# Token mixing's weight loads and masks issued ahead of the layer norm, and four expected waits reset

## The chip, the cores and the metric

The kernel runs on one core of one Trainium2 chip. The metric is the device time of one execution in microseconds (us); the median of three runs of the kernel before is 1336.76 us (1336.02 to 1337.26). A difference of about 0.2% (2.7 us) is what a measurement of this kernel can tell from none.

## What is computed

One step of a two-layer hybrid decoder over 544 positions (a prompt of 512, and 8 decode sequences of 4). In each layer one projection feeds four head groups, whose outputs are joined and projected back; a feed-forward part with a short convolution follows.

```python
def hybrid_layer(x, pos, k_pos, st, p):
    h = rmsnorm(x, p['norm1_g'])
    proj = h @ p['w_in']
    (a_qkv, a_z, a_b, a_a, b_b, b_c, b_h, c_q, c_k, c_v, d_u, d_v) = jnp.split(proj, ...)
    ...  # A: gated DeltaNet in chunks of 64; B: gated convolution; C: window attention
    du = jax.nn.gelu(d_u)
    dvn = layernorm(jax.nn.gelu(d_v), p['d_ln_g'], p['d_ln_b'])
    out_d = chunk_token_mlp(du, dvn, p['d_ws'], p['d_bias'])   # D
    x = x + jnp.concatenate([out_a, out_b, out_c, out_d], axis=-1) @ p['w_out']
    h2 = rmsnorm(x, p['norm2_g'])
    gate, f_conv_new = causal_dwconv(st['f_conv'], h2 @ p['ffn_w_gate'], p['ffn_conv_w'])
    x = x + (jax.nn.silu(gate) * (h2 @ p['ffn_w_up'])) @ p['ffn_w_down']

def chunk_token_mlp(u, v, ws, bias):
    wm = jnp.where(jnp.tril(jnp.ones((n, n), bool)), ws[:, :n, :n], 0.0)
    mixed = jnp.einsum('gts,bcsgd->bctgd', wm, vc) + bias...
    return u * mixed.reshape(bsz, t, width)
```

The change touches head group D (token mixing): a lower-triangular mask on a 128x128 weight of each of four groups, a product with the normed v rows, a bias, and a product with gelu(u).

## The kernel before

**Projections.** Activations lie with channels on the partitions. A projection of 128 columns is eight groups over the 1024 inputs; in a group each weight tile is used as a high part `wh` and a low part `wl`, in six matmuls of 272 columns (the trace shows them as three pairs, `xh,wh`, `xl,wh`, `xh,wl`). Weights come in on SP's queue (L709), ACT makes `wh` (L745) and DVE makes `wl` (L747). In a layer the projections run in the order k0 q0 v0 cq0 cq1 ck k1 q1 v1 u0 u1 c0 h0 b0 c1 h1 b1 z0 z1, then the output projection and the feed-forward part.

**Side work between the groups.** Everything else that PE does in this stage is placed between these groups by the class `Order`. Side generators (`a00` and so on for DeltaNet by layer and head pair, `c0`/`c1` for attention, `d0`/`d1` for token mixing, `n0`/`n1` for the norm of v, `g` and `e` besides) give back either a delay in planned microseconds or the name of an event; `od.mark(name, latency)` says at which planned time an event is there, and the table `LAT` adds a wait before a given step of a generator. Planned time runs with the matmuls that are issued. So the table and the marks decide PE's order at build time. The orders of DVE, ACT, POOL and SP are set afterwards by the scheduler of the build, by its own timeline; on the chip each engine runs its list in order and waits for semaphores.

**Token mixing.** `mix_d` is spawned after projection v1 and the store of the convolution state (`o_sao`, L1598). It loads `wmt` (128x512, the weights) and masks it on POOL (L1379), loads `wm4` (32x128, for the decode rows) and masks it on POOL (L1382), and loads `dbias`. Then for each of two column tiles it computes `pmx` (16 matmuls of prompt rows, from `dvn`) and `pmd` (4 of decode rows, from `dvd`), and DVE adds the bias and multiplies by `du` (`mx_`, L1399 to L1401). `normed_dv` is a generator that normalises v in five tiles: one DVE step (L1531) and two POOL steps each (L1532, L1533), then the store `o_cvs` (L1534), and marks `dv{l}`, the event for which `mix_d` waits. It is started when the projection u0 has been scaled on DVE (L1607).

**Its neighbours.** Attention makes scores `psc` (L1348 reads them, from `ck`, whose last step is L1578), exponentials on ACT (L1260), a scaling on ACT (L1268), transposes `ptr` on PE, their copies `pt` on ACT (L1363) and the product `pov`. DeltaNet makes `pk`, `pkt`, `pvt` (which needs `kd`, L1022), `pW`, `pR` and the norms `pl`, which ACT reads at L942. `psc`, `ptr`, `pl`, `pmx`, `pmd` and `pov` share one pool of two PSUM buffers, taken in turn: a matmul into it waits until the reader of the buffer's last tile is done.

Of the kernel before, what the change touches and what calls it, by code (L numbers as in the profile page):

```python
# [273 lines left out]
def _unhost(r):  # L274
# [8 lines left out]
    def conv(a, k, n):  # L283
# [19 lines left out]

LAT = {
    "a00": {
        3: 1.60, 13: 15.62, 14: 3.75, 15: 2.87, 16: 1.87, 17: 3.23, 18: 1.78, 19: 2.03, 34: 1.52,
    },
    "a01": {
        3: 3.96, 4: 1.12, 10: 2.64, 24: 0.84,
    },  # L310
    "a10": {
        3: 1.56, 13: 15.67, 14: 3.68, 15: 2.79, 16: 3.85, 17: 1.45, 25: 1.33, 36: 0.47, 42: 1.13,
    },
    "a11": {
        3: 3.59, 6: 3.32, 13: 1.06, 28: 0.70, 35: 0.30,
    },
    "c0": {
        1: 1.19, 2: 4.34, 5: 7.17, 6: 0.65, 7: 2.67, 8: 3.40,
    },
    "c1": {  # L320
        1: 0.81, 2: 4.06, 5: 7.68, 6: 0.61, 7: 15.38, 10: 1.48,
    },
    "d0": {
        4: 6.53,
# [90 lines left out]
def _body(ctx, tc, I, O, depth=DEPTH, dump=None):  # L415
# [7 lines left out]
    od = Order()  # L423

    def mm(out, lhsT, rhs, **kw):
        k, m, n = lhsT.shape[0], lhsT.free_size(), rhs.free_size()
        if lhsT.dtype == F32R:
            c = max(n, 256) / 2400.0 + 0.0025
        else:
            c = 4 * max(n, m) / 2400.0  # L430
            if k <= 32 and m <= 32:
                c *= 0.74
            elif k <= 64 and m <= 64:
                c *= 0.72
        od.spend(c, n * k / 128.0 * (1 if lhsT.dtype == F32R else 4))
        nc.tensor.matmul(out, lhsT, rhs, **kw)  # L436
# [9 lines left out]
    def bc(ap, axis, n):  # L446
        u = ap.unsqueeze(axis)
        shp = list(u.shape)
        shp[axis] = n
        return u.to_broadcast(shp)  # L450
# [16 lines left out]
    def n5(nm, w=571):  # L467
        return p5.tile([128, w], F32, tag="w5", name=nm)

    def nx(nm, shape, dt=F32):  # L470
        return slabs.tile(shape, dt, tag="s5", name=nm)

    def ncc(nm, shape):
        return pc.tile(shape, F32, tag="c2", name=nm)
# [4 lines left out]
    def ps(nm, shape):  # L479
        return pss.tile(shape, F32, tag="ps", name=nm)  # L480
# [19 lines left out]
    def C(nm, a=None, b=None):  # L500
        o, n = _COFF[nm]
        if a is None:
            return cst[:, o:o + n]
        return cst[:, o + a:o + b]
# [8 lines left out]
    def split(src, nm):  # L513
        hi, lo = nx(nm + "h", [128, T], F32R), nx(nm + "l", [128, T], F32R)
        act(hi, src, AF.Copy)  # L515
        tt(lo, src, hi.bitcast(F32), op=ALU.subtract)  # L516
        return hi, lo
# [267 lines left out]
    def dmp(nm, ap):  # L785
        if dump is not None and nm in dump:
            nc.gpsimd.dma_start(dump[nm], ap)

    def bs(ap):
        return ap.rearrange("p (b t) -> p b t", b=DB)  # L790
# [582 lines left out]


    def mix_d(l, L):
        yield ("ev", f"dv{l}")
        wmt = nx("wmt", [128, 4, 128])
        nc.sync.dma_start(wmt, I["wmt"][l])
        pool.tensor_tensor(wmt, wmt, bc(C("tri"), 1, 4), op=ALU.mult)  # L1379
        wm4 = ncc("wm4", [32, 4, 32])  # L1380
        nc.sync.dma_start(wm4, I["wm4"][l])
        pool.tensor_tensor(wm4, wm4, bc(C("udc")[0:32], 1, 4), op=ALU.mult)  # L1382
        dbias = ncc("dbias", [128, 2, 128])
        nc.sync.dma_start(dbias, I["dbias"][l])
        for i in range(2):
            yield ("ev", f"u{l}{i}")
            pmx = ps("pmx", [128, 4, 128])
            for n in range(4):
                for a in range(2):
                    gr = 2 * i + a  # L1390
                    mm(pmx[hs[a], n], L.dvn[n // 2][:, n % 2, 64 * gr:64 * gr + 64], wmt[:, gr],
                       start=True, stop=True)
            pmd = ps("pmd", [128, ND])
            for a in range(2):
                gr = 2 * i + a
                mm(pmd[hs[a]], L.dvd[0:ND, 64 * gr:64 * gr + 64], wm4[:, gr], start=True, stop=True,
                   tile_position=(0, 64 * a))
            mx_ = n5("mx_", T)
            tt(mx_[:, 0:SEQ].rearrange("p (n t) -> p n t", n=4), pmx, bc(dbias[:, i], 1, 4), op=ALU.add)  # L1399
            tt(bs(mx_[:, SEQ:T]), bs(pmd), bc(dbias[:, i, 0:DS], 1, DB), op=ALU.add)  # L1400
            tt(mx_, mx_, L.du[i], op=ALU.mult)  # L1401
            dmp(f"od{i}", mx_)
            L.cat[6 + i] = split(mx_, f"d{i}")
            yield 1.0
        od.mark(f"catD{l}", 3.5)


    def main():
# [42 lines left out]
        for l in range(depth):  # L1451
# [53 lines left out]
            for c in range(5):  # L1505
# [5 lines left out]
                dv = dvn[c // 2][:, c % 2] if c < 4 else dvd[0:ND]  # L1511
# [15 lines left out]
            def normed_dv():  # L1527
                yield ("ev", f"nd{l}")
                with tc.issue_after(L.du_ins):
                    for c, (dv, r0) in enumerate(dvs):  # L1530
                        ts(dv, dv, mv[0:r0, c, 0:1], rs[0:r0, c:c + 1], op0=ALU.subtract, op1=ALU.mult)  # L1531
                        pool.tensor_tensor(dv, dv, lnr[0:r0, 0], op=ALU.mult)  # L1532
                        pool.tensor_tensor(dv, dv, lnr[0:r0, 1], op=ALU.add)  # L1533
                nc.sync.dma_start(O["cvs"][l], dvd[0:ND])  # L1534
                od.mark(f"dv{l}", 8.0)

            od.spawn(normed_dv(), f'n{l}')
            yield 0.0

# [60 lines left out]


            od.spawn(mix_d(l, L), f'd{l}')
            L.du = []
            for i in range(2):
# [249 lines left out]
```

## Time and profile before

| | |
|---|---|
| median of three runs | 1336.76 us (1336.02 to 1337.26) |
| profiled execution | 1336.89 us, its span 1335.1 us |
| PE busy | 1291.5 us, 97% of the span |
| DVE, ACT, POOL busy | 958.9, 647.2, 401.9 us |

The profile is of one execution. PE is TensorE's matmuls; DVE, ACT, POOL and SP are VectorE, ScalarE, GpSimd and SyncE. A timeline row gives the start, the busy time, the engine, the line, the operation and its tile names, and in brackets how long the engine had stood idle before and what released it. The span begins 1.8 us later than the time that the run was measured with, or ends so much earlier.

### The profile page before, as it was taken

The page shows a single profiled execution, that of the slowest core. Times are in us where ns is not written, and L with a number is a line of the kernel's source. Part 1 is how long each engine was busy: PE and PEld are TensorE (multiplying, and loading weights), DVE is VectorE, ACT ScalarE, POOL GpSimd, SP SyncE. Part 2 cuts the span into 40 slices and gives each one's busy share as a digit, 9 for nine tenths or more (in the row PEclk, how much of TensorE's full clock was granted, in tenths as well). Part 3 has the DMA queues.
Part 4 walks back from the last instruction along what each step waited for, and adds up shares of the span by engine and source line. Part 5 has one row for each costly group of instructions (what it writes and reads, how often), then busy time and mean ns, then how long its engine had stood idle before and what let it go on. Part 6 is the DMA issues. An engine that isn't in the chain of part 4 may idle for free.

```text
span 1335.1 us, 29979 instructions
## 1 busy us (share of the span) xinstructions
PE 1291.5 (97%) x12574; PEld 1240.5 (93%) x12574; DVE 958.9 (72%) x1565; ACT 647.2 (48%) x1142; POOL 401.9 (30%) x528
## 2 busy tenths in 40 slices
PE   8998999999999999999999989999999999999997
PEld 7987889999999999999999878889989999999997
DVE  6897943579777778876658867546796887687665
ACT  6645423455455444544545543335555454455444
POOL 2123320001655354452001142100034654643321
PEclk9998999998999999999999989999999999999999
DMA  7222241231233233233532221413312332232232
GB/s 279 99 69 65 80 133 42 89 101 58 70 101 101 84 100 102 84 95 88 162 124 101 66 75 60 124 46 98 99 52 87 92 111 86 97 99 88 89 91 73
DMA packets 48086, 125.60 MB, mean 94 GB/s; under 512 B 10144, under 2 KB 14432, under 8 KB 47824
## 3 DMA queue, kind: packets, MB, share of 16 engines
q1 hardware_dynamic: 47952, 123.70, 29.6%
q8 instruction: 98, 1.61, 0.5%
q14 instruction: 36, 0.29, 0.1%
HBM read 115.01 MB, written 8.67 MB: 93 GB/s over the span
## 4 chain that ended last, share of the span: by engine, by line
PE 81%; DVE 11%; ACT 3%; issue 2%; DMA 1%; POOL 0%; SPq 0%; DVEq 0%; ACTq 0%; POOLq 0%
PE pdn L436 17%; PE pA L436 11%; PE po L436 8%; PE pD L436 7%; PE pup L436 4%; PE pgt L436 4%; PE pB L436 4%; PE pC L436 3%; DVE wl L747 3%; PE ptm L436 2%; PE pj_b L436 2%; PE pj_z L436 2%; PE pj_c L436 2%; PE pj_h L436 2%; PE p L436 2%
## 5 line engine op out<-in xcount | busy, mean ns | idle before, releaser
L747 DVE TENSOR_TENSOR wl<-wr,wh 128x1024 fp32r<-128x1024 f32 (+4 forms) x218 | 257.6, 1182 | 91.0 <-ACT wh L745 89.7
L745 ACT ACTIVATE wh<-wr 128x1024 fp32r<-128x1024 f32 (+4 forms) x218 | 194.1, 890 | 197.6 <-PE pA L436 31.0
L436 PE MATMUL pdn<-hdh,wh 128*128 128x272 f32 x684 | 142.3, 289 | 8.3 <-DVE up L1769 3.7
L436 PE MATMUL pdn<-hdl,wh 128*128 128x272 f32 x684 | 141.7, 288 | 0.5 <-DVE hdl L516 0.5
L436 PE MATMUL pdn<-hdh,wl 128*128 128x272 f32 x684 | 141.2, 288 | 0.0
L745 ACT ACTIVATE wh<-s 128x1024 fp32r<-128x1024 f32 x68 | 72.0, 1058 | 99.9 <-PE pdn L436 90.1
L724 POOL TENSOR_TENSOR s<-wr 128x512 f32<-128x512 f32 x34 | 49.7, 1463 | 228.4 <-DMA wr<-w_u 122.7
L436 PEld LDWEIGHTS pdn<-hdh,wh 128*128 128x128 f32 x684 | 107.1, 188 | 10.2 <-issue 4.4
L436 PEld LDWEIGHTS pdn<-hdl,wh 128*128 128x128 f32 x684 | 107.3, 188 | 0.9 <-DVE hdl L516 0.9
L436 PEld LDWEIGHTS pdn<-hdh,wl 128*128 128x128 f32 x684 | 107.3, 188 | 0.0
L809 DVE SCALAR_TENSOR_TENSOR cacc<-pbf,prm,cacc 128x560 f32<-128x560 f32 x88 | 82.3, 936 | 34.0 <-ACT cacc L807 33.4
L747 DVE TENSOR_TENSOR wl<-s,wh 128x1024 fp32r<-128x1024 f32 x68 | 92.0, 1353 | 8.9 <-ACT wh L745 8.4
L1694 POOL COPY sfo<-pbf 128x2 f32<-128x2 f32 x44 | 27.9, 635 | 151.6 <-DVE pbf L1760 76.2
L1795 DVE TENSOR_TENSOR xr<-xr,pdn 128x544 f32<-128x544 f32 x62 | 44.4, 715 | 40.2 <-PE pdn L436 40.2
L725 POOL TENSOR_TENSOR s<-wr,s 128x512 f32<-128x512 f32 x34 | 62.2, 1831 | 0.9
L807 ACT ACTIVATE cacc<-pbf,prm 128x560 f32<-128x560 f32 x44 | 33.6, 765 | 50.4 <-DVE pbf L1761 45.9
L726 POOL TENSOR_TENSOR s<-wr,s 128x512 f32<-128x512 f32 x34 | 57.4, 1688 | 1.4
L727 POOL TENSOR_TENSOR s<-wr 128x512 f32<-128x512 f32 x34 | 56.7, 1668 | 0.0
L800 POOL MEMSET pbf<- 128x2 f32 x44 | 4.3, 97 | 158.6 <-DVE sq L536 153.6
L516 DVE TENSOR_TENSOR hdl<-sl,hdh 128x544 fp32r<-128x544 f32 x44 | 40.1, 911 | 5.2 <-ACT hdh L515 5.2
L1700 ACT ACTIVATE sl<-cacc 128x512 f32<-128x512 f32 x44 | 27.6, 628 | 32.7 <-DVE cacc L809 32.4
L436 PE MATMUL pA<-f5h,wh 128*128 128x272 f32 x136 | 39.3, 289 | 0.0
(636 smaller groups left out, 4180.4 us busy)
## 6 DMA issues: line engine op xcount, KB each, us to landing
wr<-w_g SPq DMA_DIRECT2D x44, 512.0 KB
wr<-w_u SPq DMA_DIRECT2D x44, 512.0 KB
wr<-w_ch SPq DMA_DIRECT2D x38, 512.0 KB
wr<-w_d SPq DMA_DIRECT2D x32, 384.0 KB
wr<-w_d SPq DMA_DIRECT2D x32, 320.0 KB
wr<-w_o SPq DMA_DIRECT2D x12, 384.0 KB
xr<-x_in SPq DMA_DIRECT2D x7, 544.0 KB
wr<-w_tm SPq DMA_DIRECT2D x8, 392.0 KB
```

The source lines that it names most:

```text
L436: nc.tensor.matmul(out, lhsT, rhs, **kw)
L516: tt(lo, src, hi.bitcast(F32), op=ALU.subtract)
L724: add(s12[:, lo_], u[:, lo_], u[:, hi_], op=ALU.add)
L725: add(s12[:, hi_], g[:, lo_], s12[:, lo_], op=ALU.add)
L726: add(s43[:, lo_], g[:, hi_], s12[:, hi_], op=ALU.add)
L727: add(s43[:, hi_], g[:, lo_], u[:, lo_], op=ALU.add)
L745: act(hi, r, AF.Copy)
L747: tt(lo, r, hi.bitcast(F32), op=ALU.subtract)
L807: act(acc[:, 0:out_n], pb[:, 0:out_n], AF.Copy, scale=wcol[:, 0:1])
L809: stt(acc[:, 0:out_n], pb[:, j:j + out_n], wcol[:, j:j + 1], acc[:, 0:out_n], op0=ALU.mult, op1=ALU.add)
L1694: pool.tensor_copy(sfo[:, f, 0:2], pb[:, SEQ:SEQ + 2])
L1795: tt(xk(m), xk(m), pflat(p), op=ALU.add)
```

## The change

The event on which `mix_d` waits moves behind the three loads and the two masks, so that these are issued when `mix_d` is spawned. The mark of the norm says 11.0 us instead of 8.0. In `LAT`, the twelfth step of `a00` and `a10` (before `pvt`) waits 0.70 us of planned time, and the first step of `c0` and `c1` (before the first `psc`) 2.60 and 2.30 instead of 1.19 and 0.81.

```diff
 LAT = {
     "a00": {
-        3: 1.60, 13: 15.62, 14: 3.75, 15: 2.87, 16: 1.87, 17: 3.23, 18: 1.78, 19: 2.03, 34: 1.52,
+        3: 1.60, 12: 0.70, 13: 15.62, 14: 3.75, 15: 2.87, 16: 1.87, 17: 3.23, 18: 1.78, 19: 2.03, 34: 1.52,
...
     "c0": {
-        1: 1.19, 2: 4.34, 5: 7.17, 6: 0.65, 7: 2.67, 8: 3.40,
+        1: 2.60, 2: 4.34, 5: 7.17, 6: 0.65, 7: 2.67, 8: 3.40,
...
     def mix_d(l, L):
-        yield ("ev", f"dv{l}")
         wmt = nx("wmt", [128, 4, 128])
         nc.sync.dma_start(wmt, I["wmt"][l])
...
         nc.sync.dma_start(dbias, I["dbias"][l])
+        yield ("ev", f"dv{l}")
         for i in range(2):
...
                 nc.sync.dma_start(O["cvs"][l], dvd[0:ND])
-                od.mark(f"dv{l}", 8.0)
+                od.mark(f"dv{l}", 11.0)
```

No instruction is added or removed; the orders of all engines change between the first `psc` and the output projection of each layer, and the feed-forward parts stay as they are. Line numbers of the masks and loads are one lower after the change.

On SP in layer 0, around the stores and the loads of token mixing (`wm` is the load of `wm4`), before and then after:

```order
L709 DMA wr<-w_ch 128x1024
L1598 DMA o_sao<-sao 128x162
L709 DMA wr<-w_ch 128x1024
L1381 DMA wm_1581<-wm 32x128
L1384 DMA dbias<-dbias 128x256
L709 DMA wr<-w_ch 128x1024
L1534 DMA o_cvs<-dvd 32x256
L1378 DMA wmt<-wmt 128x512
```

```order
L709 DMA wr<-w_ch 128x1024
L1380 DMA wm_1343<-wm 32x128
L1383 DMA dbias<-dbias 128x256
L1377 DMA wmt<-wmt 128x512
L1598 DMA o_sao<-sao 128x162
L709 DMA wr<-w_ch 128x1024 x2
L1534 DMA o_cvs<-dvd 32x256
```

The three loads now stand ahead of both stores.

On PE in layer 0, from the last matmul groups of u1 to `pov` (`pj_u` and `pj_c` are groups of the projections u1 and c0), before and then after:

```order
L441 MATMUL ptr<-cst,sc 128x128 x8
L436 MATMUL pj_c_1561<-xh,wh 128x272 x2
L436 MATMUL pj_c_1561<-xl,wh 128x272 x2
L436 MATMUL pj_c_1561<-xh,wl 128x272 x2
L436 MATMUL pl_1574<-hvh,bonesr 128x512
L436 MATMUL pl_1574<-hvl,bonesr 128x512
L436 MATMUL pmx<-wmt,dvn_221 64x128 x4
L436 MATMUL pmx<-wmt,dvn_222 64x128 x4
L436 MATMUL pmd<-wm_1581,dvd 64x32 x2
L436 MATMUL pov<-pt,cv 64x256 x4
```

```order
L436 MATMUL pl_1568<-hvl,bonesr 128x512
L441 MATMUL ptr<-cst,sc 128x128 x8
L436 MATMUL pj_c_1555<-xh,wh 128x272 x2
L436 MATMUL pj_c_1555<-xl,wh 128x272 x2
L436 MATMUL pj_c_1555<-xh,wl 128x272 x2
L436 MATMUL pmx<-wmt,dvn_221 64x128 x4
L436 MATMUL pmx<-wmt,dvn_222 64x128 x4
L436 MATMUL pmd<-wm_1343,dvd 64x32 x2
L436 MATMUL pl_1612<-hvh,bonesr 128x512
L436 MATMUL pl_1612<-hvl,bonesr 128x512
L436 MATMUL pov<-pt,cv 64x256 x4
```

`ptr` moves behind the first `pl`, a second group of c0 stands ahead of `pmx`, and the next `pl` stands between `pmd` and `pov`.

On ACT in layer 0, the stretch that holds the second gelu of u (`du`) and the copies `pt`, before and then after (`sql` reads `pl`):

```order
L745 ACTIVATE wh<-wr 128x1024
L1363 ACTIVATE pt<-ptr 128x512
L1610 ACT_TABLE_LOAD
L1610 ACTIVATE du<-du 128x544
L1363 ACTIVATE pt<-ptr 128x512
ACT_TABLE_LOAD
L942 ACTIVATE sql<-pl_1574,cst 128x512
L945 ACTIVATE sql<-sql 128x512
```

```order
L745 ACTIVATE wh<-wr 128x1024
L1610 ACT_TABLE_LOAD
L1610 ACTIVATE du<-du 128x544
ACT_TABLE_LOAD
L942 ACTIVATE sql<-pl_1568,cst 128x512
L1363 ACTIVATE pt<-ptr 128x512
L945 ACTIVATE sql<-sql 128x512
L1363 ACTIVATE pt<-ptr 128x512
```

Both copies of `pt` move behind the gelu, two table loads and the step at L942; nothing else of these rows moves.

## Rows read from the trace of the kernel before

**Rows 1.** Part 4 of the page: the chain that ended last, by engine.
```profile
PE 81%; DVE 11%; ACT 3%; issue 2%; DMA 1%; POOL 0%; SPq 0%; DVEq 0%; ACTq 0%; POOLq 0%
```

**Rows 2.** PE's waits, whole span: who released it, total us, times, longest us.
```profile
PE pmx L436 <- POOL wmt L1379: 9.2, 2, 5.5
...
PE psc L436 <- DVE ck L1578: 2.7, 2, 1.4
...
PE pvt L436 <- DVE kd L1022: 1.1, 2, 0.6
```

**Rows 3.** Timeline of PE in layer 0: start, busy us, what, idle before.
```profile
79.78 0.72 PE L436 MATMUL psc<-ck,cq 64*128 64x128 f32 x8 [1.31 <-DVE ck L1578]
80.43 1.09 PE L436 MATMUL pk<-kq 64*64 64x128 f32 x16
...
115.60 0.50 PE L436 MATMUL pj_c<-xh,wh 128*128 128x272 f32 x2
...
116.44 0.39 PE L436 MATMUL pl<-hvh,bonesr 128*128 128x512 f32 x1
116.67 0.40 PE L436 MATMUL pl<-hvl,bonesr 128*128 128x512 f32 x1
122.60 1.98 PE L436 MATMUL pmx<-wmt,dvn 128*64 128x128 f32 x16 [5.54 <-POOL wmt L1379]
...
125.37 1.98 PE L436 MATMUL pov<-pt,cv 128*64 128x256 f32 x8 [0.44 <-DVE mx__1598 L1399]
```

**Rows 4.** Timeline of PE in layer 1.
```profile
777.76 1.09 PE L436 MATMUL pmx<-wmt,dvn 128*64 128x128 f32 x16 [3.64 <-POOL wmt L1379]
...
780.18 1.98 PE L436 MATMUL pov<-pt,cv 128*64 128x256 f32 x8 [0.96 <-DVE mx__9852 L1399]
```

**Rows 5.** Windows: busy us (instructions) of PE, PEld, DVE, ACT, POOL; granted clock; DMA.
```profile
123.00:130.00 7.00, 6.56 (x99) 4.91 (x96) 3.02 (x6) 1.94 (x4) 0.99 (x1) 0.50 0.01 2
...
780.00:784.00 4.00, 3.82 (x66) 2.05 (x70) 2.36 (x5) 2.21 (x4) 0.00 (x0) 0.50 0.00 2
784.00:790.00 6.00, 6.00 (x74) 5.57 (x66) 2.98 (x5) 1.59 (x4) 1.56 (x3) 0.86 0.01 3
```

**Rows 6.** Timeline of SP's queue in layer 0.
```profile
95.14 0.37 SPq L709 DMA_DIRECT2D wr<-w_ch  x1
...
118.31 0.36 SPq L1378 DMA_DIRECT2D wmt<-wmt  x1
```

**Rows 7.** Timeline of POOL in layer 0.
```profile
121.28 1.26 POOL L1379 TENSOR_TENSOR wmt<-wmt,cst 128x512 f32<-128x512 f32 x1 [3.44 <-DMA wmt<-wmt]
```

**Rows 8.** Timeline of ACT in layer 0.
```profile
115.94 0.58 ACT L1363 ACTIVATE pt<-ptr 128x512 f32<-128x512 f32 x1
116.53 1.28 ACT L1610 ACT_TABLE_LOAD   x1
118.00 0.66 ACT L1610 ACTIVATE du<-du 128x544 f32<-128x544 f32 x1 [0.18 <-DVE du L1607]
118.56 0.58 ACT L1363 ACTIVATE pt<-ptr 128x512 f32<-128x512 f32 x1
120.46 0.69 ACT L942 ACTIVATE sql<-pl,cst 128x512 f32<-128x512 f32 x1 [1.31 <-issue]
121.17 0.63 ACT L945 ACTIVATE sql<-sql 128x512 f32<-128x512 f32 x1
```

**Rows 9.** Timeline of ACT in layer 1.
```profile
777.45 0.69 ACT L942 ACTIVATE sql<-pl,cst 128x512 f32<-128x512 f32 x1 [1.31 <-issue]
```

**Rows 10.** DVE's step of the norm on the decode rows, both layers: ns min/median/max.
```profile
L1531 DVE TENSOR_SCALAR dvd<-dvd,mv,rs x2: 826/1349/1872, 112.1 to 769.5; 32x256 f32<-32x256 f32 x2
```

**Rows 11.** Windows of layer 0, columns as in rows 5.
```profile
92.00:106.00 14.00, 14.00 (x110) 12.95 (x109) 12.76 (x27) 9.14 (x19) 3.46 (x6) 1.00 0.15 50
...
142.00:156.00 14.00, 13.74 (x254) 11.53 (x253) 12.35 (x35) 2.87 (x6) 2.69 (x5) 1.00 0.33 112
156.00:170.00 14.00, 14.00 (x264) 13.42 (x263) 12.96 (x33) 7.79 (x19) 8.65 (x25) 1.00 0.24 71
```

More of the change, by code (lines that the diff above doesn't have):

```diff
@@ L311 @@
     "a10": {
-        3: 1.56, 13: 15.67, 14: 3.68, 15: 2.79, 16: 3.85, 17: 1.45, 25: 1.33, 36: 0.47, 42: 1.13,
+        3: 1.56, 12: 0.70, 13: 15.67, 14: 3.68, 15: 2.79, 16: 3.85, 17: 1.45, 25: 1.33, 36: 0.47, 42: 1.13,
     },
@@ L317 @@
     "c0": {
-        1: 1.19, 2: 4.34, 5: 7.17, 6: 0.65, 7: 2.67, 8: 3.40,
+        1: 2.60, 2: 4.34, 5: 7.17, 6: 0.65, 7: 2.67, 8: 3.40,
     },
     "c1": {
-        1: 0.81, 2: 4.06, 5: 7.68, 6: 0.61, 7: 15.38, 10: 1.48,
+        1: 2.30, 2: 4.06, 5: 7.68, 6: 0.61, 7: 15.38, 10: 1.48,
     },
```

## The prediction

> **What bounds the kernel now.** I read the shares first: PE is the chain for 81% of the span [rows 1] and is busy 97% of it, so only PE's idle time and its slow stretches are to be had. Next, PE's waits, sorted by size [rows 2]. The largest that belongs to this change is `pmx`, for the mask of `wmt` on POOL: 9.2 us in two cases, one in each layer. `psc` (2.7 us in two) and `pvt` (1.1 in two) are the small ones that the new table entries touch. Then the timeline at those places. In layer 0 PE is through with `pl` at 117.07, stands 5.54 us and starts `pmx` at 122.60 [rows 3]; in layer 1 it stands 3.64 and starts at 777.76 [rows 4]. What ended the wait: the load of `wmt` was issued only at 118.31 [rows 6], and POOL stood 3.44 us for it before the mask ran from 121.28 to 122.54 [rows 7].
>
> The stall costs more than itself. Behind it the granted clock is 0.50, the lower of the two levels, for 7 us in layer 0 and 4 us in layer 1, with 0.86 in the next 6 [rows 5]. At half clock, half of the busy time is excess: 6.56/2 = 3.3 us in layer 0, and 3.82/2 + 6.00 x 0.14 = 2.7 us in layer 1. And `pov` waits 0.44 and 0.96 for DVE [rows 3, 4]. So everything that hangs on these places is 9.2 + 1.4 + 6.0 + 2.7 + 1.1 = 20.4 us.
>
> **The change, part by part.**
>
> *Loads and masks.* The three loads now stand behind the weight load that SP issued at 95.14 [rows 6], ahead of both stores. `wmt` needed 121.28 - 118.31 = 3.0 us from issue to mask and 1.3 us for the mask [rows 6, 7], so with the smaller mask it is done by about 101 to 102, some 15 us before PE can use it. The wait for POOL goes. DMA has room there, with a share of 0.15 [rows 11]. The stores are outputs, for which no engine waits and the norm's POOL steps, which come after the masks, start only when u0 is done. I cost this part at nothing on SP and POOL.
>
> *What is late next at `pmx`.* Its two other inputs are the normed v and a free PSUM buffer. The buffer is that of `ptr`, so `pmx` waits for the first copy `pt`, and `pmd` for the second. Before, these copies ended at 116.52 and 119.14 [rows 8], hidden under the wait for `wmt`. After, they stand on ACT behind the gelu of `du`, two table loads and the step at L942. ACT was nearly without a gap there: from 115.94 to 121.15 its rows follow each other, the unrowed 1.31 before L942 being the other table load [rows 8]. The list up to L942 is otherwise the same work, so L942 ends at 121.15 less two copies of 0.58 = 119.99, and the first copy at 120.57. I take 120.6 for `pmx` in layer 0, 2.0 us before the old start.
>
> *When PE would be ready.* Counted by kind, PE does the same work ahead of the first `pmx` as before, plus one group of c0, of 116.44 - 115.60 = 0.84 us [rows 3]. The wait for `ck` was 1.31: PE was ready at 78.47, and `ck` let it go at 79.78. Now a `pk` of 1.09 and one more group (0.84) stand in front of `psc`; it is ready at about 80.4, behind `ck`, so this wait goes. For `pvt` PE comes earlier by 1.3 and later by one more group, while `kd` may come a little earlier on DVE; I leave it 0.45 of its 0.55 [rows 2]. PE is then ready for `pmx` at 117.06 - 1.31 - 0.1 + 0.84 = 116.5 and waits 120.6 - 116.5 = 4.1 us for ACT. So the gain upstream (1.4 us in each layer) is swallowed by the same wait.
>
> *Layer 0:* 2.0 us from the earlier `pmx`, 0.84 from the group already done, and 0.44 at `pov`, where a `pl` now fills the time that DVE needs: 3.3 us.
>
> *Layer 1:* here the second `pl` stands ahead of `pmx` and needs the buffer that L942 reads. L942 ended at 778.14 [rows 9]; less two copies, 776.98. PE, ready at 777.76 - 3.64 - 1.4 = 772.7, waits 4.2 us, then does `pl` (117.07 - 116.44 = 0.6), the group (0.84) and `pmx` at 778.4: 0.7 later than before, with 1.4 us of other work already done, so 0.8 us gained. `pov` keeps half of its 0.96. Layer 1: 1.3 us.
>
> *The clock.* Before, the waits of 5.54 and 3.64 us were both followed by the half clock [rows 3 to 5]. Waits of 4.1 and 4.2 us remain, so I give back nothing of the 6.0 us; if the clock holds, all of it comes on top.
>
> *What the masks do to DVE.* They move into a stretch where DVE is busy 12.76 us of 14 [rows 11], and from DVE the exponentials of ACT hang. DVE's step of the norm on the decode rows, one and the same form, took 0.83 us in one layer and 1.87 us in the other, in a stretch where POOL works on the norm too [rows 10]. If POOL is the cause, one mask can cost DVE 0 to 1.04 us, two masks up to 2.1 us in each layer. I take 0, since the norm's later steps, which the masks leave, are relieved by as much; the other end is a rival below. The Trainium skill (GPSIMD Engine Reference, Specifications) says that GpSimd shares its SBUF interfaces with VectorE, with contention for instructions that read two SBUF inputs or run in a two-port mode. The spread of 0.83 to 1.87 us agrees that something is lost, though no row here shows which port; by that rule the masks cost DVE something wherever they stand.
>
> *The rest of the stage* is reordered too (`pgb`, `pW`, the second `pmx`, the second head pair). Its waits before are small, and I take 0 with 2 us to either side.
>
> **Sum.** 1336.89 (the profiled run, 0.13 above the median, with 1.8 us outside its span) - 3.3 - 1.3 = 1332.3. I say 1332, with 1329.5 to 1334.1 for this case alone: 2 us for the rest of the stage, and a few tenths for ACT's start.
>
> **The rivals.**
>
> *The clock holds.* If the waits that remain are broken up or come out shorter, the half-clock stretch may be gone in one layer or both: 3 to 6 us more, 1326 to 1329. For it: no row shows what a wait of 2 or 3 us would do. Against it: my two are longer than the shorter of the two that had it.
>
> *Everything goes.* If ACT keeps up, because its chain begins earlier or a gap that I don't see closes, `pmx` starts when PE is ready, and 17 to 19 of the 20.4 us are saved: 1318 to 1320. ACT would have to be 4 us earlier in each layer. Against it stand the rows of ACT, which have no gap but 0.18 us [rows 8].
>
> *The gain is eaten.* The masks cost DVE the full 2.1 us a layer, the exponentials and all behind them come that much later, and of 4.6 us 0.4 is left: 1336.5. Or DVE eats it later: from 142 to 170 it is busy 25.3 of 28 us [rows 11], so PE can't run ahead by more than 2.7 us there without waiting. Either way this is 1334.1 to 1339.4, no difference that can be measured. The rule of the Trainium skill named above (GPSIMD Engine Reference, Specifications) points to the first of these.
>
> *Slower.* The place is PE right behind `pov`. Before, ACT and DVE were idle for much of the slow stretch, DVE busy 3.02 us of 7 and ACT 1.94 [rows 5], and so came to the second head pair with nothing in arrears. After, PE does its groups of c0 and the second `pl` earlier, and waits for the same chain further on, after DVE's products `mx_`, with less to put between. If that is a new wait of 3.64 us with a half-clock stretch of 2.7 us, it costs 6.3 us a layer: in one layer 1332.3 + 6.3 = 1338.6, in both 1345. The point from which it decides is 4.6 us of new waits and slow clock in all. Against it: DVE had 2.7 us free between 142 and 170, and PE was idle 0.26 us there [rows 11], so a small delay is taken up.
>
> *The change doesn't do what it says:* the loads could be held on SP by what stands ahead of them. But the order shows them behind a weight load that went out at 95.14 [rows 6], over 20 us early; the chance is nothing to speak of.
>
> **How the numbers follow.** Forecast 1332 (1329.5 to 1334.1): 0.46. Clock holds: 0.20. Everything goes: 0.10. Eaten, no difference: 0.14. Slower by over 0.2%, above 1339.4: 0.10. A difference of 0.2%, 2.7 us, is about what a measurement can tell from none; so faster (below 1334.1) is 0.46 + 0.20 + 0.10 = 0.76, same 0.14, slower 0.10. The range leaves out the case where everything goes and the slower one, 0.2 in all: 1322 to 1338.
>
> **What would show it.** `wmt`'s load and mask at about 96 and 100, and no wait of PE for POOL's mask. In its place a wait for ACT: at the first `pmx` for `pt` in layer 0, at the second `pl` for L942 in layer 1, about 4 us each, with `pmx` starting at about 119 to 121 where it was 122.60. The granted clock again 0.50 behind it. No wait at the first `psc`, and a few tenths at `pvt`. If the wait for ACT is under 2 us, or the clock stays at 1.00, the time is below 1329 and my walk along ACT is wrong; if `pmx` starts no earlier than before, or a wait of several us appears behind `pov`, it is above 1334.

## The result and the profile after

The changed kernel is slower: 1347.09 us in the median of four runs (1345.09 to 1350.58), where the kernel before, measured beside it, ran in 1337.01; the ratio is 1.0077, with a 95% interval of 1.0056 to 1.0098. That is 10 us on the other side of a forecast of 5 us faster, and outside the range.

PE's waits, over the whole span (who released it: total us, times, longest us):

```profile
PE pl L436 <- ACT sql L942: 4.4, 1, 4.4
PE pmx L436 <- ACT pt L1363: 4.2, 1, 4.2
PE pR L436 <- ACT Wc L1054: 4.1, 1, 4.1
PE py L436 <- DVE Y L1170: 3.9, 1, 3.9
...
PE pvt L436 <- DVE vnd L1225: 2.5, 1, 2.5
...
PE pkd L436 <- DVE mx__1796 L1399: 1.4, 1, 1.4
```

The wait for POOL's mask, 9.2 us before [rows 2], is gone, and so are the two at `psc`. The first two rows are the waits for ACT that the prediction put in their place. The other four were not in it: together they are 12 us, and all of them come later in the stage. The profiled run is the slowest of the four, 1350.58 us.

PE in layer 0, against [rows 3]:

```profile
80.22 0.72 PE L436 MATMUL psc<-ck,cq 64*128 64x128 f32 x8
...
120.91 1.98 PE L436 MATMUL pmx<-wmt,dvn 128*64 128x128 f32 x16 [4.22 <-ACT pt L1363]
...
124.33 1.98 PE L436 MATMUL pov<-pt,cv 128*64 128x256 f32 x8
...
134.24 1.09 PE L436 MATMUL pmx<-wmt,dvn 128*64 128x128 f32 x16
...
136.97 0.30 PE L436 MATMUL pkd<-kq 64*32 64x64 f32 x2 [1.40 <-DVE mx__1796 L1399]
...
143.47 0.26 PE L436 MATMUL py<-Y,Nd 32*32 32x32 f32 x8 [3.92 <-DVE Y L1170]
...
173.47 1.15 PE L436 MATMUL pvt<-cst,vt 64*64 64x64 f32 x32 [2.53 <-DVE vnd L1225]
```

Up to `pov` this is the forecast. `pmx` starts at 120.91 (forecast 120.6), after a wait of 4.22 us (4.1) for the copy that stands behind the gelu on ACT:

```profile
117.63 0.66 ACT L1610 ACTIVATE du<-du 128x544 f32<-128x544 f32 x1
119.59 0.69 ACT L942 ACTIVATE sql<-pl,cst 128x512 f32<-128x512 f32 x1 [1.31 <-issue]
120.18 0.59 ACT L1363 ACTIVATE pt<-ptr 128x512 f32<-128x512 f32 x1
```

The gain lasts to the second `pmx`. In the kernel before it reads:

```profile
136.78 1.09 PE L436 MATMUL pmx<-wmt,dvn 128*64 128x128 f32 x16
```

After the change it starts 2.5 us earlier, with one more group of c0 (0.84 us) done ahead of it: 3.4 us, where the forecast for layer 0 was 3.3.

Behind it comes the loss. Windows of the changed kernel (length, busy us of PE, PEld, DVE, ACT, POOL, the granted clock, DMA):

```profile
123.00:127.00 4.00, 4.00 (x76) 2.17 (x77) 2.62 (x5) 2.25 (x4) 0.00 (x0) 0.51 0.00 0
...
144.00:149.00 5.00, 5.00 (x44) 4.40 (x42) 0.95 (x3) 0.28 (x1) 0.00 (x0) 0.66 0.01 3
...
175.00:178.00 3.00, 2.99 (x31) 2.80 (x29) 2.85 (x12) 2.07 (x4) 0.00 (x0) 0.50 0.75 221
```

Behind the wait at `pmx` the clock falls to its lower level as before, and in layer 0 it falls twice more, behind the waits at `py` and `pvt`. In layer 0 that makes 1.4 + 3.9 + 2.5 us of new waits (`pkd`, `py`, `pvt`) and 5 x 0.34 + 3 x 0.50 = 3.2 us of slow clock, 11 us in all.

To compare kernels I cut the span at three starts on PE: the first `pgt` (gate projection) of layer 0, the first `psc` of layer 1, and the first `pgt` of layer 1. The last two columns are differences of such starts in one profiled execution, in us. What lies between the two stages, the feed-forward part of layer 0 and the first projections of layer 1, took 452.9 to 458.7 us, so a stage's difference is read with 2 to 3 us of doubt; the profiled runs of x4, x5 and x6 are, like that of the whole change, the slowest of their kernels. Each ratio is to runs of the kernel before that were measured beside that kernel (medians of 1337.01 to 1338.59 us).

A star marks the kernels with the later first `psc` in the table for `c1`. There a `pk` and a projection group, 1.09 + 0.84 = 1.9 us of PE's work, stand ahead of the first `psc` of layer 1 instead of behind it, so their last column is 1.9 us short against the rows without a star.

| kernel | ratio to before (95%) | layer 0 up to `pgt` | layer 1, `psc` to `pgt` |
|---|---|---|---|
| before | 1 | 281.3 | 204.4 |
| the whole change | 1.0077 (1.0056 to 1.0098) | 288.4 | 208.5* |
| x1 early loads | 0.9902 (0.9882 to 0.9923) | 275.6 | 198.0 |
| x2 table entries | 1.0085 (1.0066 to 1.0104) | 291.3 | 203.8* |
| x3 loads, entries | 1.0019 (1.0004 to 1.0034) | 288.1 | 202.7* |
| x4 loads, mark 11.0 | 0.9943 (0.9925 to 0.9961) | 275.7 | 200.5 |
| x5 loads, attention entries | 0.9928 (0.9912 to 0.9945) | 275.3 | 202.1* |
| x6 loads, DeltaNet entries | 0.9955 (0.9940 to 0.9970) | 278.2 | 206.5 |
| x7 whole change, `py` later | 0.9985 (0.9975 to 0.9994) | 279.3 | 207.8* |
| x8 as x5, `ptr` in its old place | 0.9942 (0.9924 to 0.9959) | 275.4 | 201.2* |
| x9 whole change, `ptr` earlier | 0.9970 (0.9960 to 0.9980) | 282.7 | 200.1* |
| x10 as x7, one `pR` later | 0.9987 (0.9977 to 0.9997) | 278.9 | 205.5* |
| x11 as x7, `ptr` earlier in layer 1 | 0.9955 (0.9939 to 0.9971) | 278.7 | 200.1* |
| x12 as x1, mark 8.8 | 0.9937 (0.9923 to 0.9950) | 277.5 | 202.7 |

So the whole change loses 288.4 - 281.3 = 7.1 us in layer 0 and 208.5 + 1.9 - 204.4 = 6.0 us in layer 1, 13.1 of the 13.7 us between the two profiled runs.

### The profile page after: what moved, and what is told of

Read it like the earlier page. It is cut to its first block, busy times and chain, and to the rows that moved or that the text cites. A ratio compares the mean times of both kernels' runs of the same rounds, so it can differ in the third digit from the quotient of the medians.

```text
span 1348.8 us, 29988 instructions
## 1 busy us (share of the span) xinstructions
PE 1299.2 (96%) x12574; PEld 1247.2 (92%) x12574; DVE 959.2 (71%) x1565; ACT 648.2 (48%) x1142; POOL 402.3 (30%) x528
## 4 chain that ended last, share of the span: by engine, by line
PE 83%; DVE 9%; ACT 4%; issue 3%; DMA 1%; DVEq 0%; SPq 0%; ACTq 0%
PE pdn L436 17%; PE pA L436 11%; PE po L436 7%; PE pD L436 7%; PE pup L436 5%; PE pgt L436 4%; PE pB L436 4%; PE pC L436 3%; DVE wl L747 3%; PE pj_z L436 2%; PE ptm L436 2%; PE pj_h L436 2%; PE pj_u L436 2%; PE pj_b L436 2%; PE p L436 2%
## 5 line engine op out<-in xcount | busy, mean ns | idle before, releaser
L747 DVE TENSOR_TENSOR wl<-wr,wh 128x1024 fp32r<-128x1024 f32 (+4 forms) x218 | 253.0, 1161 | 91.2 <-ACT wh L745 89.6
```

The source lines that it names most:

```text
L747: tt(lo, r, hi.bitcast(F32), op=ALU.subtract)
```

## The experiments

Theory A, formed on the trace after: the early loads are a gain, and the loss comes from the order that the planner makes of the new marks and waits, in which some matmuls stand too close behind what they need. Theory B, the rival: ACT and DVE are too full in this stage, the masks press on DVE, and the early loads are no gain by themselves. The parts of the change can be told apart cleanly, since the early loads by themselves leave PE's order word for word as it was.

### x1 to x4: the parts apart

x1 has the moved event alone, with every number as before:

```diff
     def mix_d(l, L):
-        yield ("ev", f"dv{l}")
...
         nc.sync.dma_start(dbias, I["dbias"][l])
+        yield ("ev", f"dv{l}")
```

> Only the move of the three loads and two masks ahead of the event; marks and wait table as before, so PE's order is that of the kernel before, word for word. Theory A (the loss comes from the new order of PE behind pov, through the new marks and waits): POOL's mask is done at about 101 and PE's wait for it goes; the first pmx then waits for the norm (117.84 before) and pmd for the second copy pt (119.14 before), so 3 to 5 us are saved in layer 0 and 2 to 3 in layer 1, and up to 6 us of half clock: 1325 to 1331, ratio 0.991 to 0.996. No wait at py, pkd, pR beyond 0.5 us. Theory B (the early masks press on DVE, and ACT comes late): pmx starts no more than 1 us earlier and other waits take the rest: 1335 to 1340.

The ratio is 0.9902, or 12.4 us faster than the kernel before (1325.81 against 1338.17). PE in layer 0:

```profile
117.11 1.09 PE L436 MATMUL pmx<-wmt,dvn 128*64 128x128 f32 x16
...
119.43 0.30 PE L436 MATMUL pmd<-wm,dvd 32*64 32x32 f32 x4 [1.22 <-ACT pt L1363]
...
120.57 1.27 PE L436 MATMUL pov<-pt,cv 128*64 128x256 f32 x8 [0.84 <-DVE mx__1598 L1399]
```

`pmx` does not wait at all. What is left is the wait of `pmd` for the second copy `pt`, at 119.3, as the rows of before had it [rows 8]. On POOL and DVE, in layer 0 and then in layer 1:

```profile
98.98 0.41 POOL L1381 TENSOR_TENSOR wm<-wm,cst 32x128 f32<-32x128 f32 x1 [4.25 <-DMA wm<-wm]
100.28 1.30 POOL L1378 TENSOR_TENSOR wmt<-wmt,cst 128x512 f32<-128x512 f32 x1 [0.90 <-DMA wmt<-wmt]
```

```profile
100.59 0.69 DVE L1251 TENSOR_REDUCE mx<-sc 128x2 f32<-128x512 f32 x1
101.19 0.93 DVE L910 TENSOR_TENSOR hvl<-sql,hvh 128x512 fp32r<-128x512 f32 x1
```

```profile
751.21 1.30 POOL L1378 TENSOR_TENSOR wmt<-wmt,cst 128x512 f32<-128x512 f32 x1 [1.18 <-DMA wmt<-wmt]
```

```profile
751.44 1.62 DVE L910 TENSOR_TENSOR hvl<-sql,hvh 128x512 fp32r<-128x512 f32 x1
```

The masks run beside a busy DVE. Of the steps beside them only L910 is longer than in the kernel before, where it took 0.68 us in both layers: the masks cost DVE 0.25 us in layer 0 and 0.94 us in layer 1, of the 2.1 us a layer that the prediction held possible. Against that, DVE's step of the norm on the decode rows (L1531, [rows 10]) takes 0.82 us in layer 0 of x1 where it took 1.87. Theory B falls: the early loads are a gain by themselves.

x2 has the four entries of the wait table alone:

```diff
     "a00": {
-        3: 1.60, 13: 15.62,
+        3: 1.60, 12: 0.70, 13: 15.62,
...
     "c0": {
-        1: 1.19,
+        1: 2.60,
```

(and the same in `a10` and, with 2.30, in `c1`).

> Only the four new entries of the wait table; loads, masks and mark as before. Theory A: py stands one group behind pkd in layer 0, so PE waits there 3 to 5 us for DVE's Y, with a half-clock stretch behind it, while the wait for POOL's mask stays at 4 to 5 us: slower than before, 1339 to 1348, ratio 1.002 to 1.008. Theory B: the wait at psc goes and nothing else changes for the worse: 1333 to 1337.

The ratio is 1.0085. PE's two longest waits in layer 0, then the longest of layer 1:

```profile
PE pmx L436 <- POOL wmt L1379: 7.8, 1, 7.8
PE py L436 <- DVE Y L1170: 3.6, 1, 3.6
```

```profile
PE pmx L436 <- ACT pt L1363: 7.0, 1, 7.0
```

The entries alone cost 12 us, more than expected: the wait at `py` is there, and the waits at `pmx` are longer than before (5.54 and 3.64), in layer 1 for ACT's copy.

x3 is x1 and x2 together.

> Early loads and masks with the four new entries; the mark stays at 8.0. Theory A: the gain of the early loads (5 to 11 us) and the loss of the order (5 to 10) stand against each other: 1332 to 1341, 4 to 12 us above the run with the early loads alone, with the wait at py of 3 to 5 us. Theory B: no faster than the new entries alone.

The ratio is 1.0019, 15 us above x1 and so a little more than expected. `py` waits 3.6 us and `pmx` 5.0 in each layer, now for ACT's copies. Beside x1 this says that the waits for ACT that the prediction saw are not left over once the mask is early: they come with the entries.

x4 is x1 with the mark of 11.0.

> Early loads and masks with the mark of 11.0; wait table as before. Theory A, as far as it names the table entries: py has its 18 rows behind pkd, so no wait there; pmx is planned later, so the time is within 4 us of the run with the early loads alone. If the mark has a part in the loss, a new wait shows behind pov and the time is 1333 or more. Theory B: as with the early loads alone, 1335 to 1340.

The ratio is 0.9943, some 5.6 us above x1. No wait at `py`; in layer 0 the stage is as short as in x1 (275.7), in layer 1 it is 2.5 us longer, where `pvt` waits 2.1 us for `kd`; that is less than half of the 5.6 us, and no run here places the rest. The mark has a part in the loss. On top of the entries it costs more: from x3 to the whole change, which differ by the mark alone, the ratio rises from 1.0019 to 1.0077, 8 us, and nearly all of it is in layer 1 (202.7 to 208.5), where waits of 5.0 us at `pmx` and 1.3 at `pR` become 4.4 at `pl` and 4.1 at `pR`. So of the 23 us that the new order costs against x1, 15 come with the entries and 8 with the mark.

### x5 and x6: which entries

x5 is x1 with the two attention entries (`c0`, `c1`), x6 is x1 with the two DeltaNet entries (`a00`, `a10`).

> Early loads and masks, and of the wait table only the two entries of attention (first psc later). PE's order from u1 to the second head pair stays that of the kernel before; py has 15 rows behind pkd. If it takes both pairs of entries to bring about the loss: the two waits at psc (2.7 us) go and nothing comes in their place, so 0 to 3 us below the early loads alone (ratio to before 0.988 to 0.991). If the attention entries alone cause it (they put the first gelu of u ahead of the silu of v on ACT): 4 us or more above the early loads alone, with a wait of PE for ACT at pmx or pt.

> Early loads and masks, and of the wait table only the two entries of DeltaNet (pvt later). Here pov stands ahead of pmx, and two pl stand together. If it takes both pairs: within 3 us of the early loads alone (ratio 0.989 to 0.993), pvt waits less than 0.3 us, py does not wait. If the DeltaNet entries alone cause the loss: 4 us or more above, with new waits behind u1.

The ratios are 0.9928 and 0.9955, both above x1, by 3 and 7 us; the 3 us are at the limit of what the measurement can tell. In neither does `py` wait over 0.2 us in layer 0; that takes both pairs. In x5 layer 0 is as in x1 (275.3) and layer 1 is 202.1 + 1.9 - 198.0 = 6.0 us longer: there `ptr` stands one group later, the second gelu goes ahead of `pt` on ACT, `pmx` waits 3.5 us, and a later `ptr` 1.7. In x6 it is `ptr` that waits for DVE's scaling (2.2 and 3.3 us), and `pmd` (1.1 and 2.4). So neither pair gives back the waits that it is there to remove, 2.7 and 1.1 us; the DeltaNet pair clearly costs more, and the attention pair does so in the profile of layer 1.

### x7, x10, x11: mending the whole change

x7 is the whole change with one more entry, between `pkd` and `py`:

```diff
     "e0": {
-        4: 6.92,
+        4: 6.92, 5: 5.00,
```

> The whole change, with one more entry in the wait table: 5.00 us of planned time between pkd and py (e0, step 5), so that py stands behind three groups of h0, pk, ptr, pR and two more groups. Theory A (the order that the planner makes from too short a wait at py is the loss in layer 0): the wait of 3.9 us at py and the half clock behind it go, 5 to 8 us below the whole change (1339 to 1342, ratio to before 1.001 to 1.005), while the waits for ACT at pmx and pl stay at 4 us. If the chain on DVE is late in itself, the wait moves to the next of its readers and the time stays above 1344.

The ratio is 0.9985, against 1.0077 for the whole change, more than the 5 to 8 us that were expected, and layer 0 falls from 288.4 to 279.3 us. The waits at `py` and at `pvt` for `vnd` are both gone, and the slow stretches behind them too; the wait of 4.2 us at `pmx` stays, as expected. One number that PE's planner lacked was worth 9 us in layer 0.

x10 adds an entry for the wait of layer 1, `pR` for ACT's copy `Wc`:

```diff
     "a10": {
-        17: 1.45, 25: 1.33,
+        17: 1.45, 20: 4.50, 25: 1.33,
```

> The whole change, with the entry for py (5.00) and one more, 4.50 us between pW and the last pR of layer 1's first head pair (a10, step 20), where PE waited 4.05 us for ACT's copy Wc in the whole change and 4.6 with the entry for py. The wait and the half clock behind it go: 4 to 8 us below the whole change with the entry for py alone, 1328 to 1333, ratio to before 0.992 to 0.996; the waits for ACT at pmx and pl stay. If it only moves on: above 1334.

The expectation failed: 0.9987, no faster than x7. The wait at `pR` went, and another of 3.2 us stood further on:

```profile
PE pst L436 <- DVE vnb L1227: 3.2, 1, 3.2
```

x9 mends something earlier, the place of `ptr`, by cutting the wait ahead of the second `psc` (step 5 of `c0` from 7.17 to 5.00, of `c1` from 7.68 to 5.50) in the whole change:

> The whole change, with the wait before the second psc (step 5 of c0 and c1) cut to 5.00 and 5.50 and nothing else, so that ptr, pov and what follows stand earlier; on ACT the copies pt stand ahead of the second gelu again, and py has 17 rows behind pkd in layer 0. If the copies' place on ACT makes the waits at the first pmx and the second pl: these fall from 4.2 and 4.4 us to under 1.5, and with the one at py the time comes to 1326 to 1333, ratio to before 0.991 to 0.996. If ACT is late whatever the order: waits of 3 us or more for ACT stay there, above 1336.

The ratio is 0.9970, a little above what was expected. In layer 1 it holds: the waits at `pl` and `pR`, 4.4 and 4.1 us, become 1.5 and none, and the stage falls from 208.5 to 200.1 us. In layer 0 the copies are early too and the wait of `py` is gone, but now `ptr` comes too early for its own input, three times, and `pmd` has to wait for its buffer:

```profile
PE ptr L441 <- DVE sc L1270: 4.4, 2, 3.1
PE pmd L436 <- ACT oc L1371: 1.7, 1, 1.7
PE ptr L441 <- ACT sc L1268: 1.4, 1, 1.4
```

x11 takes from each the layer where it helped: the entry for `py`, and step 5 of `c1` at 5.50.

> The whole change with two entries mended, one for each layer: 5.00 us between pkd and py (e0, step 5), which alone took layer 0 from 288.4 to 279.3 us, and in layer 1 the second psc 2.18 us earlier in the plan (c1, step 5: 5.50), which with its twin took layer 1's mixing from 208.5 to 200.1. If the whole change loses by these two places: layer 0's mixing ends at 279 to 280, layer 1's takes 199 to 202, and the time is 1327 to 1332, ratio to before 0.992 to 0.996, some 16 us below the whole change. If the loss is spread over many small places: 1334 or more, since mending two of them can't give it back.

The ratio is 0.9955, 1331.85 us, with stages of 278.7 and 200.1: inside what was expected, and 0.0122 (16 us) below the whole change. Two places carry 16 of the 23 us, `py` in layer 0 and `ptr` in layer 1. What still lies between x11 and x1 is 3 us in layer 0, where `pmx` keeps its wait of 4.2 us, and 200.1 + 1.9 - 198.0 = 4 us in layer 1.

### x8 and x12: two attempts to beat x1

x8 is x5 with step 5 of `c0` and `c1` cut by what the attention entries add (5.77 and 6.37), so that only the first `psc` and the first `ptr` of each layer stand later and everything from u1 on stands on PE as in x1.

> Early loads and masks, the two new entries of attention, and the wait before its second psc (step 5 of c0 and c1) cut by as much as the new entries add (5.77 and 6.37 instead of 7.17 and 7.68), so that only the first psc moves and ptr stands where it stood before in both layers. If ptr's shift was what the attention entries cost in layer 1 (pt behind the second gelu on ACT, 3.5 us at pmx): the waits at psc go (2.7 us), no wait above 1.5 us at pmx, 1 to 3 us below the early loads alone, ratio to before 0.986 to 0.990. If the gelu ahead of the silu on ACT is what costs: no better than the early loads with the attention entries, 0.992 to 0.994.

The gain that was expected did not come: the ratio is 0.9942, no better than x5, as the second branch had it. The waits at `psc` are gone and come back as waits of `pmx` (1.1 us) and `pmd` (1.4) for ACT's copies and of `pvt` for `kd` (1.2), in both layers. PE came earlier, and ACT and DVE did not; whether the gelu ahead of the silu on ACT is the reason, no run separates.

x12 is x1 with a mark of 8.8, so that one group of c0 comes between `pl` and the first `pmx`; behind that, much of the stage shifts by about a group.

> Early loads and masks with the old wait table and a mark of 8.80 instead of 8.0 (or 11.0): one group of c0 comes between pl and the first pmx in both layers, and nothing else moves until the second head pair. With the early loads alone PE waited 1.22 and 0.88 us at pmd for the second copy pt, and 0.84 and 0.54 at pov. If these waits are what is left to take: pmd's goes, pov's stays, 1 to 3 us below the early loads alone, ratio to before 0.987 to 0.991. If the order behind pov suffers as with the mark of 11.0: 0.992 or more.

The gain that was expected did not come here either: the ratio is 0.9937. The wait at `pmd` shrank to 0.26 us, and `pov` now waits 3.59 us in layer 0 and 3.6 in layer 1, for DVE's `mx_`. DVE of x12 and then of x1 in layer 0:

```profile
121.33 0.69 DVE L948 TENSOR_TENSOR kq<-kq,sql 128x512 f32<-128x512 f32 x1 [2.04 <-ACT sql L945]
121.94 0.68 DVE L1399 TENSOR_TENSOR mx__1604<-pmx,dbias 128x512 f32<-128x512 f32 x1
```

```profile
119.84 0.68 DVE L1399 TENSOR_TENSOR mx__1598<-pmx,dbias 128x512 f32<-128x512 f32 x1
...
121.98 0.69 DVE L948 TENSOR_TENSOR kq<-kq,sql 128x512 f32<-128x512 f32 x1 [1.37 <-ACT sql L945]
```

With `pmx` one group later in the build, the scheduler put L948 ahead of `mx_` on DVE. L948 waits for ACT, and `mx_`, whose input was there, stands behind it for 2 us. x1 has the lowest ratio of all kernels here; its interval overlaps that of x5.

## Why the prediction was wrong

**What bounds the kernel** was read rightly: taking away the wait for the mask, and nothing else, is worth 12.4 us (x1), of 9.2 + 6.0 us that the prediction put down to the waits and the slow clock behind them.

**Loads and masks** at no cost: right. In the changed kernel the masks of layer 0 are done at 101.4, and no step of DVE beside the masks is longer than before, in either layer. In x1, where other steps stand beside them, DVE lost 0.25 and 0.94 us. On the rule of the Trainium skill (GPSIMD Engine Reference, Specifications) the trace of x1 agrees: beside the mask, L910 with two SBUF inputs was longer, while L1251, a reduction with one, kept its 0.69 us. The prediction's bound of 2.1 us a layer was not reached in any of these, and that the masks cost DVE something wherever they stand is not what the changed kernel shows.

**The waits for ACT**: right in kind and size (4.22 and 4.40 us measured, 4.1 and 4.2 forecast), and so was the half clock behind them. The prediction read the reason off the new order, the copies' place behind the gelu on ACT. It did not ask what puts them there. x1 and x4 show that it isn't the early mask: with the old wait table no such wait is left (`pmx` does not wait, and `pl` 0.9 us at most). It is the new table entries, which move `ptr` behind `pl` in the plan, and with it the copies `pt` on ACT.

**The rest of the stage** is the step that failed. The prediction took "0 with 2 us to either side" for everything behind `pov`; it was a loss of some 11 us in layer 0, and in layer 1 of some 7 us, the 6.0 us by which the stage grew and the 1.3 us of gain that was forecast. In layer 1 it is a wait of 4.1 us at `pR` with a slow stretch behind it, one of 0.9 at `pkd`, and a slow stretch behind the wait at `pl` that is longer than the one before:

```profile
788.00:794.00 6.00, 5.56 (x35) 4.01 (x34) 2.96 (x6) 2.25 (x5) 0.00 (x0) 0.50 0.05 20
...
829.00:838.00 9.00, 4.95 (x104) 4.43 (x100) 7.62 (x27) 4.10 (x13) 0.00 (x0) 0.75 0.33 110
```

The prediction's ground was that the waits there were small before, and that DVE had 2.7 us free between 142 and 170. Neither bears on it. Free time says what an engine can do in a stretch, not how long a chain takes through it. In the kernel before, DVE and PE around `pkd` and `py` read:

```profile
139.67 0.30 PE L436 MATMUL pkd<-kq 64*32 64x64 f32 x2
...
146.63 0.26 PE L436 MATMUL py<-Y,Nd 32*32 32x32 f32 x8
```

```profile
142.96 0.24 DVE L1167 SCALAR_TENSOR_TENSOR Nd<-pkd,nbeta,De 128x32 f32<-128x32 f32 x1
...
146.31 0.18 DVE L1170 TENSOR_TENSOR Y<-Y,cst 128x32 f32<-128x32 f32 x1
```

From `pkd` to `Y` it is 6.8 us, since `mx_`, `wl` and others stand between on DVE, and PE had 7.0 us of work to put there: `pkd` itself, four groups of h0, `pk`, `pR` and `ptr`. No wait showed, because two things that have nothing to do with each other came out alike. The planner's own number for this distance is 1.5 us. After the change:

```profile
138.88 0.25 DVE L1167 SCALAR_TENSOR_TENSOR Nd<-pkd,nbeta,De 128x32 f32<-128x32 f32 x1
...
142.08 1.24 DVE L1170 TENSOR_TENSOR Y<-Y,cst 128x32 f32<-128x32 f32 x1
```

The chain takes 143.3 - 137.0 = 6.3 us, no longer than before; but PE has only `pkd`, `pW` and one group of h0 to put in it, and waits 3.92 us. This could have been worked out ahead of the result: PE's order is fixed when the kernel is built, and the old trace had the 6.8 us. With `py` mended, layer 0 of x11 is 281.3 - 278.7 = 2.6 us shorter than in the kernel before, near the forecast of 3.3.

Layer 1's `pR` is of the same kind. `pW` ended at 826.5, and ACT's copy of it stood behind a weight copy, the exponentials, a step that waited for DVE, and the scaling:

```profile
825.79 0.69 PE L436 MATMUL pW<-R,N 32*32 32x32 f32 x32
...
833.76 1.07 PE L436 MATMUL pR<-Wc,Tm 32*32 32x32 f32 x64 [4.05 <-ACT Wc L1054]
```

```profile
828.34 0.51 ACT L1260 ACTIVATE sc<-sc,nm 128x256 f32<-128x256 f32 x1
...
832.15 0.91 ACT L1268 ACTIVATE sc<-sc,es 128x256 f32<-128x256 f32 x2
832.96 0.74 ACT L1054 ACTIVATE Wc<-pW 32x256 f32<-32x256 f32 x2
```

Moving `pR` alone gave nothing (x10). Moving `ptr`, with which the exponentials go, took this wait away as well (x9, x11). I read that as the head of the chain, but no run separates `ptr` from the steps that move with it, so for layer 1 this part of the cause stays open.

**The rivals.** The slower one came nearest: PE behind `pov`, new waits with less work to put between, a slow stretch behind them, and 1345 for both layers. That the time fits is in part luck. It priced one wait of 3.64 us for DVE's `mx_` at 6.3 us a layer; the waits for `mx_` are 1.4 and 0.9 us, at `pkd`, the larger ones hang on chains that it didn't name (`Y`, `vnd`, `Wc`), and the price was 11 us in layer 0 and 7 in layer 1. Its chance of 0.10 was too low, because it was weighed by DVE's free time. "Everything goes" needed ACT 4 us earlier in each layer; with the old wait table the first copy `pt` of layer 0 does end at 116.8 (x1), 3.9 us ahead of the changed kernel, but the time was 1325.81 and not 1318 to 1320, as the waits at `psc` and `pvt` and a slow stretch are left.

**The table entries** were costed at their own waits, 2.7 and 1.1 us, "swallowed" upstream. They cost 12 us by themselves (x2), because each moves all that comes after it in its generator, and with that the order against the other generators.

## What to carry to other kernels

When a change alters the order of one engine, list each matmul that now stands closer behind what it needs, take the latency of that chain from the old trace, and subtract the work that the new order leaves between them; free time on the other engines is no answer to that. A move that leaves the order alone (an earlier load) and a move that changes it (a wait in a planner) should be tried apart, since the first can hide the second's cost: here the early loads gave 12 us, and the new order cost 23. An expected wait that is set "as the trace has it" is true of one order only, and the waits of zero in that trace may be luck that the next order takes away.

## What the runs showed of the hardware

The slow stretch did not come only behind the long waits. In x1, where PE waited 1.22 and 0.84 us within 3 us, the windows behind show a granted clock of 0.86 and 0.87; in layer 1, with waits of 0.88 and 0.54, it stayed at 1.00:

```profile
117.00:123.00 6.00, 3.94 (x94) 2.74 (x94) 4.63 (x7) 3.92 (x6) 1.83 (x3) 0.86 0.31 106
123.00:130.00 7.00, 7.00 (x103) 6.22 (x104) 4.73 (x9) 2.77 (x5) 1.12 (x2) 0.87 0.01 4
...
772.00:778.00 6.00, 6.00 (x113) 4.99 (x110) 3.83 (x6) 3.76 (x8) 1.88 (x3) 1.00 0.21 76
778.00:784.00 6.00, 6.00 (x155) 5.34 (x155) 5.08 (x16) 1.88 (x3) 0.00 (x0) 1.00 0.29 85
```

So with 2.1 us of waits came 6 x 0.14 + 7 x 0.13 = 1.8 us of slow clock, and with 1.4 us none. It is one case of each.

One small step of DVE, L1170 on 128x32 elements, took 1.24 us in the changed kernel (from 142.08) instead of 0.18, while POOL was at work on 128x512 elements:

```profile
141.55 1.73 POOL L971 TENSOR_TENSOR qk<-qk,cst 128x512 f32<-128x512 f32 x1
```

It lay on the chain that PE waited for at `py`. It does not make that wait: in x2 and x3 the same step took 0.18 and 0.17 us, and `py` waited 3.6 us all the same.
